# Top-k over 112 candidate sums instead of 256, and V's gate and activation tiles in a pool of their own that opens before U ends

## The chip, the cores and the metric

The kernel runs on 1 core of one Trainium2 chip. The metric is device time in microseconds (us) for one launch, the median of several runs; less is better. Engines are named as in the profile: PE (matrix multiply), PEld (its weight loads), DVE (vector), ACT (scalar), POOL (GpSimd) and SP, which here only issues DMAs. ACTq, SPq and POOLq are the DMA issues in the instruction streams of ACT, SP and POOL.

## What is computed

Two layers of a transformer step on 640 tokens of width 1024, handled as five tiles of 128 tokens (four latent tiles, n = 0 to 3, and one context tile, PT = 4). Each layer has a mixer and then a product-key expert retrieval ("PEER"), which is most of the time and all of the change:

```
q   = (x @ w_q) as 8 heads x 2 halves of 64
sc  = q . sub_keys                       # 128 scores for each token, head and half
sv, si = top_k(sc, 16)                   # 16 best of 128, each half, sorted
cand = sv[half 0][:, None] + sv[half 1][None, :]     # 16 x 16 sums
cv, ci = top_k(cand, 16)                 # 16 best of 256
i1, i2 = si[half 0][ci // 16], si[half 1][ci % 16]
idx  = i1 * 128 + i2                     # one of 16384 experts
gate = softmax(cv)
act  = gelu(u[idx] . x)                  # 8 x 16 = 128 experts for each token
out  = sum over experts of gate * act * v[idx]
```

Both lists of 16 are sorted in falling order. A pair (a, b), with a the rank in half 0 and b in half 1, has at least (a+1)(b+1) pairs (itself among them) with sums no smaller, so a pair can be among the best 16 only where (a+1)(b+1) <= 16. For a < 4 that allows b up to 15, and for a >= 4 it allows b <= 2.

## The kernel before

For the four latent tiles the retrieval is not a gather but dense, in two phases. **U**: for each of 128 chunks of 128 experts, PE multiplies the chunk of u (128x1024) with all 512 latent tokens, three products of hi/lo halves (24 matmuls of 512 columns a chunk), ACT takes the gelu into a tile `ga`, and ACT's queue stores it to DRAM (`gad[c]`). **V**: for each chunk the stored activations are loaded again (tile `gr`), multiplied on DVE with the chunk's gates (tile `gate`, loaded from the DRAM array `Gd`, four chunks a tile), split into hi and lo (tile `whl`, ACT then DVE), and PE multiplies them with the chunk of v (`vh`, `vl`) into eight PSUM banks over all 128 chunks. The weights of either phase come as `raw` and `x` tiles, which live through both phases and are shared, as are their splits `hl`. The context tile uses gathers instead: 128 indirect DMAs by POOL of rows of u (`gather_u`, during U) and of v (`gather_v`, during V), each followed by one pass of DVE.

Where the gates come from: `pick` (line 960) runs once for each of the five tiles. POOL adds the 16 x 16 sums of all 8 heads (line 966), `top16` (lines 953 to 958) makes five DVE passes over each head's sums, small DVE operations split ci into ranks, and for each half DVE compares with a row of 0 to 15 (line 978), POOL multiplies (line 980) and DVE sums (line 981). ACT takes the exponential (line 985). `build_gate` (line 991) turns a tile's result into dense gates: DVE makes one-hot rows E and M (line 1006), PE multiplies them in, ACT copies the product to `stg`, and ACT's queue stores that to `Gd`. The picks of tiles PT and 0 stand ahead of U in the program; the gates of tiles 0 to 3, with the picks of tiles 1 to 3 woven in, are spread over U's chunks 4 to 107 (lines 1201 to 1231).

SBUF is handed out in pools on a stack, by default from the left. Those that matter, in layer l: `q` (through U and V), `a` (`hn`, `ga`, `gth`; U only), `tt` (the picks and gates; until chunk 111 of U, ASPLIT = 112), then `ta` (modulation blocks in four `wm` buffers, in layer 0 alone, two `rowb` rows; the last 16 chunks of U), then after U's last chunk `a` is released and `v` opened, with everything V needs: `gate` 2 buffers of 8 KB a partition, `gr` 6 of 2 KB, `whl` 4 of 4 KB, `gth`, `wm` and `rowb`. The first users of a pool wait until what lay at its place is done.

The order of instructions on each engine and DMA queue is fixed when the program is built: a planner runs through the program with its own costs and, at each point, puts on an engine the earliest instruction in program order that is ready. The chip then runs each engine's list in that order and waits where an operand is late. In V, `issue_after` also ties the multiplication of chunk c to come after the lo split of chunk c - 2 in DVE's list (line 1084).

Of the kernel before, what the change touches and what calls it, by code (L numbers as in the profile page):

```python
# [33 lines left out]
GLD = 4  # L34
# [43 lines left out]
def build(tc, nc, I, O, dbg=None):  # L78
# [39 lines left out]
    def phase(name, wide):  # L118
        if extra[0]:
            extra[0].release()  # L120
        PA[0] = wide
        extra[0] = name and tc.alloc_tile_pool(name=name, bufs=1, space=PSUM, reuse_waits="tile")
# [299 lines left out]
    def mod_steps(P, blocks, bufs):  # L422
        sB = mod_rows(P)
        for l, b in blocks:
            mod_block(P, l, b, sB, bufs)
            yield
# [526 lines left out]
    def top16(s, v, i):  # L953
        V.max(v[:, 0:8], s)  # L954
        V.max_index(i[:, 0:8], v[:, 0:8], s)  # L955
        V.match_replace(s, v[:, 0:8], s, LOWEST)  # L956
        V.max(v[:, 8:16], s)
        V.max_index(i[:, 8:16], v[:, 8:16], s)

    def pick(P, n, sv, si, i1, i2, gt):  # L960
        sif = P.tile([128, 8, 2, 16], F32, name="sif", bufs=1)
        V.tensor_copy(sif, si)
        cv = P.tile([128, 8, 16], F32, name="cv", bufs=1)
        ci = P.tile([128, 8, 16], U32, name="ci", bufs=1)
        cand = P.tile([128, 8, 16, 16], F32, name="cand", bufs=1)
        G.tensor_tensor(cand, sv[:, :, 0, :, None].to_broadcast([128, 8, 16, 16]),
                        sv[:, :, 1, None, :].to_broadcast([128, 8, 16, 16]), OP.add)
        for h in range(8):
            top16(cand[:, h].rearrange("p a b -> p (a b)"), cv[:, h, :], ci[:, h, :])
            yield  # L970
        ab = P.tile([128, 2, 8, 16], U32, name="ab", bufs=1)
        V.tensor_single_scalar(ab[:, 0], ci, 4, OP.logical_shift_right)
        V.tensor_single_scalar(ab[:, 1], ci, 15, OP.bitwise_and)
        abf = P.tile([128, 2, 8, 16], F32, name="abf", bufs=1)
        V.tensor_copy(abf, ab)
        for j, dst in ((0, i1), (1, i2)):
            eq = P.tile([128, 8, 16, 16], F32, name="cand", bufs=1)
            V.tensor_tensor(eq, abf[:, j, :, :, None].to_broadcast([128, 8, 16, 16]),  # L978
                            iota16[:, None, None, :].to_broadcast([128, 8, 16, 16]), OP.is_equal)
            G.tensor_tensor(eq, eq, sif[:, :, j, None, :].to_broadcast([128, 8, 16, 16]), OP.mult)  # L980
            V.tensor_reduce(dst.rearrange("p (h k) -> p h k", h=8), eq, axis=AX.X, op=OP.add)  # L981
            yield
        g3 = gt.rearrange("p (h k) -> p h k", h=8)
        V.tensor_sub(g3, cv, cv[:, :, 0:1].to_broadcast([128, 8, 16]))
        S.activation(gt, gt, AF.Exp)
        z = P.tile([128, 8], F32, name="z", bufs=2)
        V.reduce_sum(z, g3, axis=AX.X)
        V.reciprocal(z, z)
        V.tensor_mul(g3, g3, z[:, :, None].to_broadcast([128, 8, 16]))
# [76 lines left out]
                V.scalar_tensor_tensor(accp, t, dots[:, k:k + 1], accp, op0=OP.mult, op1=OP.add)  # L1066
            yield

    def v_phase(l, P, pv, Gd, gad, steps, mods, finish):
        ws, gt, lows = {}, {}, []  # L1070

        def load_gate(g):
            gt[g] = P.tile([128, 16, GLD, 32], F32, name="gate", bufs=2)
            cc = g * GLD % 64
            load(gt[g], Gd[:, g * GLD // 64, :, cc * 32:(cc + GLD) * 32].rearrange("u p (c t) -> p u c t", c=GLD))

        def prep(c):
            ga = P.tile([128, 512], F32, name="gr", bufs=6)
            load(ga, gad[c])
            if c == 0:  # L1080
                load_gate(0)
            if (c + GAHEAD) % GLD == 0 and c + GAHEAD < NCH:
                load_gate((c + GAHEAD) // GLD)
            with tc.issue_after(lows[-2].ins) if c > 1 else contextlib.nullcontext():
                V.tensor_mul(ga.rearrange("p (u t) -> p u t", t=32), ga.rearrange("p (u t) -> p u t", t=32),  # L1085
                             gt[c // GLD][:, :, c % GLD, :])
            w = P.tile([128, 2, 512], F32R, name="whl", bufs=4)
            lows.append(split(w[:, 0], w[:, 1], ga))
            raw = chunk_tile(c)
            load(raw, I["vC"][l, :, c, :])  # L1090
            vh, vl = hl_tile(), hl_tile()
            split(vh, vl, raw, V)
            ws[c] = (w, vh, vl)
            if True:
                next(steps, None)
                if c % 16 == 15:
                    next(steps, None)
                if c >= MOD0 and (c - MOD0) % 2 == 0:
                    next(mods, None)

        def use(c, n):
            w, vh, vl = ws[c]
            ns = slice(n * 128, (n + 1) * 128)
            p0, q0 = pv[n]
            a, z = c == 0, c == NCH - 1
            h0, h1 = slice(0, 512), slice(512, 1024)
            mm(p0, w[:, 0, ns], vh[:, h0], a, False)
            mm(q0, w[:, 0, ns], vh[:, h1], a, False)
            mm(p0, w[:, 0, ns], vl[:, h0], False, False)
            mm(q0, w[:, 0, ns], vl[:, h1], False, False)  # L1110
            mm(p0, w[:, 1, ns], vh[:, h0], False, z)
            mm(q0, w[:, 1, ns], vh[:, h1], False, z)

        def back(n):
            xs[n] = x_tile(n)
            load(xs[n], xm[l][n])

        for c in range(NCH - TAIL):
            prep(c)
            if c == XLAST:  # L1120
                back(PT)
            for n in range(NL):
                use(c, n)
        for c in range(NCH - TAIL, NCH):
            prep(c)
        for n in range(NL):
            back(n)
        finish(-1)
        E = mybir.EngineType
        with tc.manual_schedule(engines={E.PE, E.DVE, E.Activation, E.Pool}):  # L1130
            for i in range(NL + 2):
                for n in {0: (0,), 1: (1,), 2: (2, 3)}.get(i, ()):
                    for c in range(NCH - TAIL, NCH):
                        use(c, n)
                finish(i)
# [26 lines left out]
    for l in range(DEPTH):  # L1162
# [8 lines left out]
        with tc.tile_pool(name=f"q{l}", bufs=1) as Q:  # L1171
# [9 lines left out]
            with tc.tile_pool(name=f"t{l}", bufs=1) as TP:  # L1181
# [6 lines left out]
                with tc.tile_pool(name=f"tt{l}", bufs=1) as R:  # L1188
# [39 lines left out]
                                next(bg, None)  # L1228
                    for _ in bg:
                        pass  # L1230
            with tc.tile_pool(name=f"ta{l}", bufs=1) as R:
                mods = mod_steps(R, [(0, b) for b in range(40, 48)], 4) if l == 0 else iter(())
                for c in range(ASPLIT, NCH):
                    nc.scalar.dma_start(gad[c], a_chunk(A, l, c))
                    with tc.issue_after(pace[0].ins):
                        next(steps, None)
                    next(mods, None)
                for g in range(2):
                    gate_row(rows[g], l, g, 40, p2())
            A.release()  # L1240
            with tc.tile_pool(name=f"v{l}", bufs=1) as R:
                phase(f"psV{l}", 1)
                wide = [p2(), p2()]
                pv = [(pacc(), pacc()), (p1(), p1())] + [(t[:, :512], t[:, 512:]) for t in wide]
                if dbg and "f" in dbg:
                    load(dbg["f"][l, PT], accp)
                jobs, lgb = {}, []

                def step(n):
                    if n == PT and n not in jobs:  # L1250
                        lgb.extend(bc_row(R.tile([128, D], F32, name="rowb", bufs=2), I[k][l, 1]) for k in ("ln_g", "ln_b"))
                    if n not in jobs:
                        f = (accp,) if n == PT else (pv[n] if n < 2 else (wide[n - 2],))
                        jobs[n] = close_layer(l, R, n, f, rows[grp_of(n)], *lgb)
                    next(jobs[n], None)

                def finish(i):
                    if i < 0:
                        for _ in range(5):
                            step(PT)  # L1260
                        return
                    tile = lambda k: PT if k == -1 else (k if 0 <= k < NL else None)
                    for k in (i - 2, i, i - 1, i, i - 2, i, i - 1, i - 2):
                        if tile(k) is not None and (k >= 0 or i > 0):
                            step(tile(k))

                v_phase(l, R, pv, Gd, gad, gather_v(R, l, idx, gp, dots, accp),
                        mod_steps(R, [(1, b) for b in range(48)], 2) if l == 0 else iter(()), finish)
    phase(None, 0)
    ps_pool.release()  # L1270
    dram.release()
# [99 lines left out]
```

## Time and profile before

| what | value |
|---|---|
| median of 3 runs | 4023.82 us (4019.87 to 4028.7) |
| the profiled execution | 4019.37 us, of which its span is 4017.6 us |
| PE busy | 3791.2 us, 94% of the span |
| DVE busy | 3068.7 us, 76% |
| ACT busy, POOL busy | 1435.9 us (36%), 1218.5 us (30%) |
| mean granted PE clock | 0.969 of full |
| DMA | 934.02 MB, mean 232 GB/s |

Layer 0 has its U from about 517 to 1327.5 us of the span and its V from 1350 to about 2045; layer 1 has them from about 2473 to 3282 and from 3303 on. A busy PE is not PE at its full rate: a matmul counts as busy at either clock.

### The profile page before, as it was taken

What the parts mean: (1) busy time and instruction counts of PE and PEld (TensorE: products, weight loads), DVE (VectorE), ACT (ScalarE), POOL (GpSimd) and SP (SyncE); (2) the same over time, 40 slices, a digit from 0 to 9 for tenths busy, and PEclk for the clock granted to TensorE, in tenths of its full rate; (3) what the DMA queues carried; (4) which work ended last, traced back from release to release, by engine and by line L of the source; (5) the groups of instructions that cost most, each with busy time, mean ns of one, the idle gap of its engine ahead of it and who ended that gap; (6) DMA issues with size and microseconds to landing.
All of it is one profiled execution on the core that took longest, in us unless ns stands there. A gap on an engine that the chain in (4) does not pass through costs nothing. (4 is left out here: it accounts for less than half of the span.)

```text
span 4017.6 us, 52309 instructions
## 1 busy us (share of the span) xinstructions
PE 3791.2 (94%) x18606; PEld 3091.6 (77%) x18606; DVE 3068.7 (76%) x5984; ACT 1435.9 (36%) x2201; POOL 1218.5 (30%) x946
## 2 busy tenths in 40 slices
PE   6799999999999799999999999999999979999998
PEld 5577777777888688888877778777788868888886
DVE  6867799999766588988765659999986537778545
ACT  5443532333333222222344553323343322222222
POOL 5412445442111222322141243553211113343100
PEclk7899999999999899999999999999999989999999
DMA  6223248777888899999831132677788869999763
GB/s 224 79 71 118 84 139 280 251 256 272 292 263 299 298 350 346 342 343 344 261 103 52 58 106 91 237 262 246 243 307 275 263 223 341 348 340 345 251 195 104
DMA packets 405623, 934.02 MB, mean 232 GB/s; under 512 B 32624, under 2 KB 166896, under 8 KB 397168
## 3 DMA queue, kind: packets, MB, share of 16 engines
q1 hardware_dynamic: 280656, 517.34, 39.4%
q0 software_dynamic: 73728, 268.47, 19.0%
q10 hardware_dynamic: 50976, 144.87, 9.7%
q8 instruction: 146, 2.39, 0.2%
q14 instruction: 117, 0.96, 0.1%
HBM read 785.06 MB, written 145.49 MB: 232 GB/s over the span
## 5 line engine op out<-in xcount | busy, mean ns | idle before, releaser
L83 PE MATMUL pa<-Hhi,hl 128*128 128x512 f32 x4096 | 1318.7, 400 | 11.6 <-ACT ga L1044 11.5
L83 PE MATMUL p<-hl,whl 128*128 128x512 f32 x4608 | 1089.3, 390 | 0.0
L83 PEld LDWEIGHTS p<-hl,whl 128*128 128x128 f32 x4608 | 867.5, 188 | 180.3
L83 PEld LDWEIGHTS pa<-Hhi,hl 128*128 128x128 f32 x4096 | 778.9, 191 | 181.5 <-ACT ga L1044 13.9
L83 PE MATMUL pa<-Hlo,hl 128*128 128x512 f32 x2048 | 815.0, 398 | 0.0
L199 ACT ACTIVATE hl<-x 128x1024 fp32r<-128x1024 f32 x284 | 301.3, 1061 | 960.2 <-PE p L83 578.1
L1061 POOL DMA_INDIRECT gth<-v,idx x256 | 361.0, 1410 | 825.2 <-DVE accp L1066 593.6
L199 ACT ACTIVATE hl<-raw 128x1024 fp32r<-128x1024 f32 x292 | 309.0, 1059 | 775.5 <-PE pa L83 373.7
L200 DVE TENSOR_TENSOR hl<-x,hl 128x1024 fp32r<-128x1024 f32 x272 | 345.3, 1270 | 265.6 <-ACT hl L199 260.6
L200 DVE TENSOR_TENSOR hl<-raw,hl 128x1024 fp32r<-128x1024 f32 x246 | 331.2, 1347 | 238.3 <-ACT hl L199 236.2
L83 PEld LDWEIGHTS pa<-Hlo,hl 128*128 128x128 f32 x2048 | 391.3, 191 | 81.5
L83 PE MATMUL pa<-hl,Hhi 128*128 128x512 f32 x1232 | 438.5, 424 | 7.6 <-DVE gtmp L914 2.8
L83 PE MATMUL pa<-hl,whl 128*128 128x512 f32 x1536 | 391.7, 390 | 43.5 <-DMA gr<-gad 22.6
L83 PEld LDWEIGHTS pa<-hl,whl 128*128 128x128 f32 x1536 | 289.2, 188 | 104.2 <-issue 23.0
L1066 DVE SCALAR_TENSOR_TENSOR accp<-gth,dots,accp 128x1024 f32<-128x1024 f32 x254 | 325.3, 1281 | 4.5 <-DMA gth<-v,idx 2.7
L1050 POOL DMA_INDIRECT gth<-u,idx x128 | 165.9, 1296 | 462.9 <-DVE gth L1052 404.9
L1050 POOL DMA_INDIRECT x<-u,idx x128 | 168.9, 1320 | 448.7 <-DVE x L1052 425.6
L83 PEld LDWEIGHTS pa<-hl,Hhi 128*128 128x128 f32 x1232 | 235.4, 196 | 54.9 <-DVE gtmp L914 3.7
L83 PE MATMUL pa<-hl,Hlo 128*128 128x512 f32 x616 | 260.6, 423 | 14.3 <-POOL Hlo L200 10.5
L1006 DVE TENSOR_TENSOR M<-E,g 128x1024 f16<-128x1024 f16 x256 | 189.3, 771 | 58.7 <-PE p L83 57.7
L1024 ACT ACTIVATE stg<-p 128x512 f32<-128x512 f32 x256 | 138.9, 597 | 233.8 <-PE p L83 153.2
L1085 DVE TENSOR_TENSOR gr<-gr,gate 128x512 f32<-128x512 f32 x256 | 175.2, 685 | 24.7 <-DMA gate<-Gd 24.7
(339 smaller groups left out, 4635.6 us busy)
## 6 DMA issues: line engine op xcount, KB each, us to landing
x<-v SPq DMA_DIRECT2D x158, 512.0 KB
raw<-uT SPq DMA_DIRECT2D x130, 512.0 KB
gad<-ga ACTq DMA_DIRECT2D x256, 256.0 KB
Gd<-stg ACTq DMA_DIRECT2D x64, 1024.0 KB
gr<-gad SPq DMA_DIRECT2D x256, 256.0 KB
gate<-Gd SPq DMA_DIRECT2D x64, 1024.0 KB
x<-uT SPq DMA_DIRECT2D x126, 512.0 KB
raw<-v SPq DMA_DIRECT2D x98, 512.0 KB
```

Source lines behind the costliest of these rows:

```text
L83: return T.matmul(out, l, r, start=start, stop=stop, skip_group_check=True)
L199: S.activation(hi, src, AF.Copy)
L200: return (eng or V).tensor_sub(lo, src, hi.bitcast(F32))
L1006: V.tensor_tensor(out, src, col.rearrange("p (q r) -> p q r", r=2)[:, :, None, :].to_broadcast(shape), op)
L1024: S.activation(st[a][:, :, b * 8:(b + 1) * 8], v[:, a], AF.Copy, scale=1.0 / GSCALE)
L1050: G.indirect_dma_start(out=t, out_offset=None, in_=I["u"], in_offset=bass.IndirectOffsetOnAxis(ap=idx[:, k:k + 1], axis=0))
L1061: G.indirect_dma_start(out=t, out_offset=None, in_=I["v"], in_offset=bass.IndirectOffsetOnAxis(ap=idx[:, k:k + 1], axis=0))
L1066: V.scalar_tensor_tensor(accp, t, dots[:, k:k + 1], accp, op0=OP.mult, op1=OP.add)
L1085: V.tensor_mul(ga.rearrange("p (u t) -> p u t", t=32), ga.rearrange("p (u t) -> p u t", t=32), gt[c // GLD][:, :, c % GLD, :])
```

## The change

`pick` adds 4 x 16 sums of the first four ranks (columns 0 to 63 of a head) and 12 x 4 of the other twelve (columns 64 to 111), in two POOL instructions instead of one, and `top16` runs over 112 columns instead of 256. The ranks are then found from the column c: a = max(c >> 4, (c >> 2) - 12), and b = c - min(16 a, 4 a + 48). V's `gate` and `gr` tiles move out of `v` into a pool `H` on the right-hand side, opened after `tt` is released and before `ta`; the other tiles of V stay in `v`. The modulation blocks in `ta` get two buffers instead of four.

```diff
-        cand = P.tile([128, 8, 16, 16], F32, name="cand", bufs=1)
-        G.tensor_tensor(cand, sv[:, :, 0, :, None].to_broadcast([128, 8, 16, 16]),
-                        sv[:, :, 1, None, :].to_broadcast([128, 8, 16, 16]), OP.add)
+        cand = P.tile([128, 8, 256], F32, name="cand", bufs=1)[:, :, :112]
+        for a0, a1, nb in ((0, 4, 16), (4, 16, 4)):
+            shape = [128, 8, a1 - a0, nb]
+            part = cand[:, :, :64] if a0 == 0 else cand[:, :, 64:]
+            G.tensor_tensor(part.rearrange("p h (a b) -> p h a b", b=nb),
+                            sv[:, :, 0, a0:a1, None].to_broadcast(shape),
+                            sv[:, :, 1, None, :nb].to_broadcast(shape), OP.add)
         for h in range(8):
-            top16(cand[:, h].rearrange("p a b -> p (a b)"), cv[:, h, :], ci[:, h, :])
+            top16(cand[:, h], cv[:, h, :], ci[:, h, :])
             yield
...
-        V.tensor_single_scalar(ab[:, 1], ci, 15, OP.bitwise_and)
+        V.tensor_single_scalar(ab[:, 1], ci, 2, OP.logical_shift_right)
         abf = P.tile([128, 2, 8, 16], F32, name="abf", bufs=1)
         V.tensor_copy(abf, ab)
+        cf = P.tile([128, 8, 16], F32, name="cif", bufs=1)
+        V.tensor_copy(cf, ci)
+        V.scalar_tensor_tensor(abf[:, 0], abf[:, 1], -12.0, abf[:, 0], op0=OP.add, op1=OP.max)
+        V.tensor_scalar(abf[:, 1], abf[:, 0], 4.0, 48.0, op0=OP.mult, op1=OP.add)
+        V.scalar_tensor_tensor(abf[:, 1], abf[:, 0], 16.0, abf[:, 1], op0=OP.mult, op1=OP.min)
+        V.tensor_sub(abf[:, 1], cf, abf[:, 1])
...
-            gt[g] = P.tile([128, 16, GLD, 32], F32, name="gate", bufs=2)
+            gt[g] = H.tile([128, 16, GLD, 32], F32, name="gate", bufs=2)
...
-            ga = P.tile([128, 512], F32, name="gr", bufs=6)
+            ga = H.tile([128, 512], F32, name="gr", bufs=6)
...
+            H = tc.alloc_tile_pool(name=f"h{l}", bufs=1, side="right")
             with tc.tile_pool(name=f"ta{l}", bufs=1) as R:
-                mods = mod_steps(R, [(0, b) for b in range(40, 48)], 4) if l == 0 else iter(())
+                mods = mod_steps(R, [(0, b) for b in range(40, 48)], 2) if l == 0 else iter(())
...
+            H.release()
```

## Rows read from the trace of the kernel before

**Rows 1.** Stretches: us; busy (count) of PE, PEld, DVE, ACT, POOL; PEclk, DMA, GB/s.

```profile
640.00:905.00 265.00, 243.68 (x1214) 194.79 (x1213) 262.60 (x458) 87.15 (x121) 126.06 (x62) 0.96 0.74 254
905.00:1327.50 422.50, 415.52 (x2360) 338.75 (x2358) 298.57 (x428) 156.79 (x234) 75.82 (x62) 1.00 0.80 275
1327.50:1350.10 22.60, 0.01 (x1) 0.01 (x1) 2.72 (x4) 4.41 (x6) 4.68 (x5) 0.59 0.90 291
1400.00:1950.00 550.00, 550.00 (x2428) 455.56 (x2427) 482.45 (x652) 159.65 (x202) 156.17 (x109) 1.00 0.98 342
2595.00:2880.00 285.00, 259.28 (x1290) 207.31 (x1289) 284.94 (x471) 92.43 (x129) 132.37 (x65) 0.95 0.73 246
```

**Rows 2.** Waits of PE, whole run: us in total, times, longest.

```profile
PE p L83 <- DVE M L1006: 40.1, 18, 3.9
PE pa L83 <- ACT ga L1044: 11.5, 4, 5.4
```

**Rows 3.** Timeline at layer 0's change from U to V: start, us, engine, instruction [idle].

```profile
1328.89 0.33 ACTq L1234 DMA_DIRECT2D gad<-ga  x1
...
1331.24 0.33 SPq L1079 DMA_DIRECT2D gr<-gad  x1
...
1349.39 0.63 ACT L199 ACTIVATE whl<-gr 128x512 fp32r<-128x512 f32 x1 [10.81 <-DVE gr L1085]
...
1350.12 2.04 PE L83 MATMUL pa<-hl,whl 128*128 128x512 f32 x4 [22.61 <-DMA gr<-gad]
```

**Rows 4.** The same of layer 1.

```profile
3285.59 0.33 SPq L1079 DMA_DIRECT2D gr<-gad  x1
...
3302.30 0.63 ACT L199 ACTIVATE whl<-gr 128x512 fp32r<-128x512 f32 x1 [18.86 <-DVE gr L1085]
...
3302.98 2.08 PE L83 MATMUL pa<-hl,whl 128*128 128x512 f32 x4 [20.90 <-ACT whl L199]
```

**Rows 5.** Timeline of SP's queue in layer 0: the first load for V.

```profile
1274.07 0.33 SPq L1090 DMA_DIRECT2D raw<-v  x1
```

**Rows 6.** Timeline of layer 0's U: last modulation block, first gate row.

```profile
1275.11 0.16 DVE L429 TENSOR_TENSOR modT<-modT,bmod 128x2 f32<-128x2 f32 x1
...
1284.31 1.02 ACT L439 ACTIVATE g2row<-p 128x1024 f32<-128x1024 f32 x1
```

**Rows 7.** Waits of ACT in V of layer 0, 1400 to 1950 us.

```profile
ACT hl L199 <- PE p L83: 389.8, 101, 3.9
```

**Rows 8.** Instructions on tile cand: duration ns min/median/max, first and last start us, forms.

```profile
L954 DVE MAX8 cv<-cand x80: 401/406/425, 550.7 to 2812.0; 128x8 f32<-128x256 f32 x80
...
L955 DVE FIND_INDEX8 ci<-cv,cand x80: 408/420/439, 553.4 to 2818.1; 128x8 uint32<-128x256 f32 x80
...
L980 POOL TENSOR_TENSOR cand<-cand,sif x20: 4567/4964/6827, 571.1 to 2871.4; 128x2048 f32<-128x2048 f32 x20
...
L966 POOL TENSOR_TENSOR cand<-sv x10: 3670/3694/3797, 547.0 to 2801.5; 128x2048 f32<-128x2048 f32 x10
```

**Rows 9.** The same for tile sc, whose passes run over 128 columns.

```profile
L954 DVE MAX8 sv<-sc x160: 274/331/584, 453.4 to 2497.6; 128x8 f32<-128x128 f32 x160
...
L955 DVE FIND_INDEX8 si<-sv,sc x160: 290/350/598, 454.6 to 2499.9; 128x8 uint32<-128x128 f32 x160
```

**Rows 10.** Groups of DVE, 480 to 1010 us: busy us, mean ns | idle.

```profile
L975 DVE CAST abf<-ab 128x256 f32<-128x256 uint32 x5 | 1.5, 303 | 0.0
```

**Rows 11.** Timeline at the start of tile 2's pick, layer 0.

```profile
762.51 3.69 POOL L966 TENSOR_TENSOR cand<-sv 128x2048 f32<-128x2048 f32 x1 [1.42 <-DVE i L981]
762.55 4.80 DVE L1006 TENSOR_TENSOR M<-E,g 128x1024 f16<-128x1024 f16 x2
...
766.81 0.23 PE L83 MATMUL p<-M,E 128*128 128x128 f16 x1 [1.38 <-DVE M L1006]
```

**Rows 12.** Timeline of ACT at the context tile's pick, layer 0 and layer 1.

```profile
568.00 0.31 ACT L985 ACTIVATE gp<-gp 128x128 f32<-128x128 f32 x1 [8.70 <-DVE gp L984]
...
2523.89 0.31 ACT L985 ACTIVATE gp<-gp 128x128 f32<-128x128 f32 x1 [10.13 <-DVE gp L984]
```

More of the change, by code (lines that the diff above doesn't have):

```diff
@@ L1067, in gather_v, with v_phase @@
             yield
-    def v_phase(l, P, pv, Gd, gad, steps, mods, finish):
+    def v_phase(l, P, H, pv, Gd, gad, steps, mods, finish):
         ws, gt, lows = {}, {}, []
         def load_gate(g):
-            gt[g] = P.tile([128, 16, GLD, 32], F32, name="gate", bufs=2)
+            gt[g] = H.tile([128, 16, GLD, 32], F32, name="gate", bufs=2)
             cc = g * GLD % 64
@@ L1265, in finish @@
                             step(tile(k))
-                v_phase(l, R, pv, Gd, gad, gather_v(R, l, idx, gp, dots, accp),
+                v_phase(l, R, H, pv, Gd, gad, gather_v(R, l, idx, gp, dots, accp),
                         mod_steps(R, [(1, b) for b in range(48)], 2) if l == 0 else iter(()), finish)
+            H.release()
     phase(None, 0)
```

## The prediction

> **What bounds the kernel now.** I read the page's busy times first, then the stretches, then who PE waits for, then the timelines where it waits. PE is the engine to watch: in V it is busy without a gap for 550 of 550 us at full clock [rows 1]. It loses time in two kinds of place in each layer. At the change from U to V it stands still for 22.6 us in layer 0 and 20.9 us in layer 1 [rows 3, 4]. And in the stretch of U where the picks and gates are made it is busy for 243.7 of 265 us in layer 0 and 259.3 of 285 us in layer 1, while DVE is busy for 262.6 and 284.9 us of these: DVE sets the pace there, and PE loses 21.3 and 25.7 us [rows 1], mostly to the one-hot rows M (40.1 us in 18 waits over the run, [rows 2]). The two parts of the change fall on these two places.
>
> **The change of phase.** The last chunk's store is issued at 1328.89, and the first load of `gr` goes out 2.35 us later, at 1331.24 [rows 3]: that is when the pool `v` opens. All that follows is a chain of load, multiplication and split, which ends in ACT's hi split at 1349.39 and PE's start at 1350.12. With `gate` and `gr` in `H`, the loads and the first two multiplications can run during U's last chunks, and the chain from the opening is only the split, since `whl` still lies in `v`: 1350.12 - 1349.39 = 0.73 us. So PE starts at about 1331.24 + 0.73 = 1331.97 instead of 1350.12 and saves 18.1 us. In layer 1 it starts at 3285.59 + (3302.98 - 3302.30) = 3286.27 instead of 3302.98 and saves 16.7 us [rows 4]. Sum: 34.8 us, with bounds 0 (the planner leaves the loads where they are) and 34.8. I take the upper end, because the planner already issues loads of V when a place is free: the first of v's chunks goes out at 1274.07, 53 us before U's end [rows 5]. I leave 2 us off for V's first chunks, where DVE must now also take in the first gathered rows of v while PE is already running. The clock I leave alone: it is at a mean of 0.59 over the idle stretch [rows 1], and a remaining gap of 4 us may still bring it to its lower level.
>
> What is moved costs this. SP gets eight loads ahead of U's last ones, six of 256 KB and two of 1 MB, 3.5 MB or 10.2 us at the 342 GB/s of V [rows 1]. In U's last 422 us the DMA engines are busy to 0.80 [rows 1], so some 84 us are free, and these loads hide there; a u chunk that comes later by 10 us is covered by the chunks already split (ten `hl` tiles, two a chunk). DVE gets two multiplications more before U's end, where it is busy for 298.6 of 422.5 us [rows 1], so they cost nothing. With two `wm` buffers instead of four the eight modulation blocks may take longer; they end at 1275.11, and the first row made of them is copied at 1284.31 [rows 6], which gives 9.2 us of cover. Bounds 0 and some 5 us; I take 0.
>
> **The picks.** MAX8 takes at least 401 ns over 256 columns and 274 over 128, FIND_INDEX8 408 and 290 [rows 8, 9]: 122 ns for 128 columns, so 138 ns for the 144 that go. There are 5 passes (the other three taken alike) x 8 heads = 40 a tile: 5.5 us. The five added operations have half the width of the cast at line 975, which takes 303 ns [rows 10]: between 0.5 and 1.5 us, of which I take the upper end. Net 4.0 us of DVE time a tile. The sums on POOL go from 2048 elements in 3.69 us [rows 8] to 896 in two instructions: 1.6 us by their number, 3.7 if a short inner row of 4 costs what it saves; I take 1.7, nearest to the row by its time an element. That matters to DVE, since it stands while POOL adds: at 762.55 two M operations are begun and end 1.15 us after POOL's 3.69 us are over, and PE, which needs an M, waits 1.38 us [rows 11]. So another 2.0 us a tile (bounds 0 and 2.1). Together 6.0 us a tile, 30 us a layer, 60 us in all, of DVE time. POOL's two products at line 980 (4.96 us each, [rows 8]), which halt DVE as well, stay.
>
> [...]
>
> How much reaches PE? Tiles 1 to 3 lie in the stretch where DVE sets the pace: 18 us a layer. If DVE's list were the only limit, PE's loss of 21.3 and 25.7 us would fall by 18 each. If the waits came from the halts by line 980 alone, they would stay. I take 11 a layer, a little over half, since DVE has no idle time there to absorb a halt: 22 us. Tiles PT and 0 lie ahead of it, where PE waits only at the context tile's exponential. ACT waits for it for 8.70 and 10.13 us with everything behind it in its list, the gelu among it [rows 12], and PE for up to 5.4 us of that (11.5 us in four waits, [rows 2]), so 10.13 - 5.4 = 4.7 us are covered. DVE's chain ahead of it gets 5.5 + 2.0 = 7.5 us shorter, but the planner, which sees a shorter chain too, may put the exponential earlier. Between 0 and 11.5 us; I take 5.
>
> **Sum.** 34.8 - 2 + 22 + 5 = 60 us. The profiled execution took 4019.4 us, 4.4 less than the median of the three runs; from it 3959.4 comes out, from the median 3963.8. I say 3961.
>
> **Rivals.**
> - The picks' relief doesn't reach PE, because the halts by line 980 set its waits: the change of phase alone, 33 us, 3987 us. For it: the waits are short (40.1 us in 18) and each can follow a halt. Against it: DVE has no idle time in between. 0.14.
> - All of it does: 34.8 - 2 + 36 + 11.5 = 80 us, 3940 us. For it: DVE busy for 284.9 of 285 us. 0.13.
> - V of layer 0 is bound by the DMA engines (busy to 0.98 there), so an earlier start ends it earlier only by the 3.5 MB already loaded, 10.2 us instead of 18.1: 3969 us. Against it: ACT's splits wait 389.8 us for PE to free tiles, in 101 waits, and for no DMA [rows 7]. 0.07. [...]
> - The change doesn't do what it says: the loads stay behind U's end, for want of a place or by the planner's order. With the picks' 27 us 3994 us (0.04); with little of these either about 4020 us (0.03).
> - Slower: the exponential moves ahead on ACT. Its place in ACT's list comes from the planner's costs, and there are five a layer, of which one now makes PE wait. If each of the ten waited W us, PE would lose 10 x (W - 4.7), against some 10 now. It decides from W = 4.7 + (34.8 - 2 + 22 + 10)/10 = 11.2 us; at W = 13 PE would lose 83 us and the kernel would take about 4039 us. For it: both such waits of today are near it (8.7 and 10.1). Against it: the chain on DVE gets shorter, and the later tiles' exponentials cause no wait today. 0.05.
>
> **How the numbers follow.** My forecast has 0.54, with a range of its own of 3945 to 3978. The rivals' 3940, 3969, 3987 and 3994 are all faster by more than 0.2% (8 us, about what a measurement of this kernel can tell from no change): 0.54 + 0.14 + 0.13 + 0.07 + 0.04 = 0.92; within 0.2% 0.03; slower 0.05. The range for 8 in 10 reaches from 3931, where the clock also gives something back, to 3994.
>
> **What would show it.** Right: loads of `gr` and `gate` on SP's queue some 50 us or more before U's end, PE idle for 4 to 6 us at both changes of phase, MAX8 over 112 columns at about 0.26 us, the sums on POOL at 1.6 to 2.0 us in two parts, and fewer waits of PE for M. Wrong: `gr` loads that start with `v`; PE idle again a few chunks into V, on `whl` or a load; new waits of ACT at line 985; a DVE stretch as long as before. If U's waits are unchanged, the second part of the sum fails; if V waits for DMAs, the first.

## The result, and the profile after

The changed kernel took 3981.72 us (median; 3979.86 to 3985.91), the kernel before beside it 4021.85 us. The ratio is 0.9899, with a 95% interval of 0.9882 to 0.9916: 40 us, or 1.0%, less. 3961 was predicted, so the gain is two thirds of the 60 us forecast. The profiled execution took 3980.8 us, 38.6 less than that of before; its span is 3979.0 us.

I give the stretches between the starts of the first and last matmul of each phase, and PE's idle time between the phases, read from the two traces, since the page shows only sums over the run:

| stretch | before | after | difference |
|---|---|---|---|
| U, layer 0 | 826.3 | 830.0 | +3.7 |
| PE's wait from U to V, layer 0 | 22.6 | 4.4 | -18.2 |
| V, layer 0 | 699.5 | 699.7 | +0.2 |
| U, layer 1 | 824.9 | 817.6 | -7.3 |
| PE's wait from U to V, layer 1 | 20.9 | 4.2 | -16.7 |
| V, layer 1 | 698.5 | 698.5 | 0 |

The stretches of the changed kernel that answer to [rows 1], and one more, 1216 to 1250 us, columns as there:

```profile
640.00:905.00 265.00, 245.86 (x1370) 197.19 (x1369) 263.82 (x508) 95.72 (x139) 100.02 (x61) 0.98 0.75 259
905.00:1330.00 425.00, 414.81 (x2231) 338.55 (x2231) 267.04 (x390) 149.54 (x218) 69.65 (x61) 0.99 0.81 276
...
1216.00:1250.00 34.00, 25.66 (x107) 20.44 (x105) 15.41 (x24) 11.31 (x12) 5.76 (x5) 0.90 1.05 367
1400.00:1950.00 550.00, 550.00 (x2428) 455.44 (x2427) 485.76 (x647) 159.59 (x202) 163.97 (x113) 1.00 0.98 345
2595.00:2880.00 285.00, 267.19 (x1557) 215.22 (x1556) 283.68 (x541) 109.60 (x163) 95.42 (x59) 0.98 0.77 265
```

V is what it was: 2428 matmuls in 550 us before and after. In the stretch of the picks DVE is as full as before (263.8 of 265 us). New are 34 us, 80 us before the end of layer 0's U, in which PE is busy for only 25.7, at a clock of 0.90.

PE's waits over the whole run, to be set beside [rows 2]:

```profile
PE p L83 <- DVE M L1016: 33.4, 20, 3.9
PE pa L83 <- ACT ga L1054: 22.0, 8, 8.1
...
PE pa L83 <- ACT whl L199: 8.6, 2, 4.4
```

The waits for M fell by 6.7 us only. Those for the gelu's tile `ga` doubled, and one of them is 8.1 us long.

The change from U to V in the timeline, layer 0 and then layer 1, beside [rows 3, 4]:

```profile
1218.73 0.43 SPq L1089 DMA_DIRECT2D gr<-gad  x1
...
1332.16 0.33 ACTq L1245 DMA_DIRECT2D gad<-ga  x1
...
1334.45 0.63 ACT L199 ACTIVATE whl<-gr 128x512 fp32r<-128x512 f32 x1 [2.32 <-DMA gad<-ga]
...
1335.18 1.19 PE L83 MATMUL pa<-hl,whl 128*128 128x512 f32 x2 [4.40 <-ACT whl L199]
...
3263.68 1.15 ACT L199 ACTIVATE whl<-gr 128x512 fp32r<-128x512 f32 x2 [2.17 <-DMA gad<-ga]
...
3264.36 2.07 PE L83 MATMUL pa<-hl,whl 128*128 128x512 f32 x4 [4.20 <-ACT whl L199]
```

`gr` is loaded from 1218.73 on, 112 us before U ends (1330.78). What is left of the chain is what the prediction left: `v` opens when the last store has freed its place, 2.3 us after that was issued, and PE starts 0.73 us after ACT's split (1335.18 - 1334.45).

The timeline of the new stall, on SP, ACT and PE:

```profile
1216.83 1.86 SPq L308 DMA_DIRECT2D wm<-wmodT  x2
1218.73 0.43 SPq L1089 DMA_DIRECT2D gr<-gad  x1
1220.10 0.38 SPq L1085 DMA_DIRECT2D gate<-Gd  x1
1221.05 9.54 SPq L1089 DMA_DIRECT2D gr<-gad  x1
...
1223.80 0.58 ACT L1054 ACTIVATE ga<-pa 128x512 f32<-128x512 f32 x1
1235.51 0.33 ACTq L1233 DMA_DIRECT2D gad<-ga  x1
1235.87 1.28 ACT L302 ACT_TABLE_LOAD   x1 [11.49 <-DMA gate<-Gd]
...
1242.08 0.79 PE L83 MATMUL pa<-Hhi,hl 128*128 128x512 f32 x1 [8.05 <-ACT ga L1054]
```

The gelu of a chunk ends at 1224.4, but its store goes out at 1235.51, and what ended ACT's 11.49 us of idle time is the landing of the first `gate` load, issued at 1220.10 on SP. The store has no data in common with that load. In the trace the DMAs of SP and ACT take their completion semaphores (the counters that tell that a transfer has landed) from one set of eight in turn (numbers 100 to 104, 106, 109 and 110 in the issues from 1216.78 us on), and the store's is the one that the `gate` load holds, number 109: ACT's wait for it ends at 1235.45. But for its own gelu the store waits for nothing else. The load is 1 MB and lands only after 15.4 us (1220.10 to 1235.51), at a time when `wm`, `rowb`, `gate` and `gr` loads are under way together (DMA share 1.05 in the stretch). ACT waits in its issue of the store. Behind it in ACT's list stand a split, the work on the `rowb` rows and two table loads (1.28 us each), so the next gelu comes only at 1241.42, and PE with it.

In layer 1 the store of the same chunk waits in the same way, but its semaphore, number 102, is held by a `gr` load of 256 KB issued at 3159.53. ACT's wait is 6.21 us, and no work on `rowb` follows:

```profile
3172.72 1.06 ACT L199 ACTIVATE hl<-raw 128x1024 fp32r<-128x1024 f32 x1 [6.21 <-DMA gr<-gad]
```

There PE has no wait from 3140 to 3200 us.

The exponentials: tile 0's in ACT's timeline of the kernel before, to be set beside [rows 12],

```profile
625.61 0.31 ACT L985 ACTIVATE gt<-gt 128x128 f32<-128x128 f32 x1 [4.45 <-DVE gt L984]
```

and ACT's timeline and then PE's of the changed kernel:

```profile
557.50 0.31 ACT L995 ACTIVATE gp<-gp 128x128 f32<-128x128 f32 x1 [4.51 <-DVE gp L994]
...
600.98 0.31 ACT L995 ACTIVATE gt<-gt 128x128 f32<-128x128 f32 x1 [9.21 <-DVE gt L994]
...
604.20 0.79 PE L83 MATMUL pa<-Hhi,hl 128*128 128x512 f32 x1 [4.46 <-ACT ga L1054]
...
2546.01 0.80 PE L83 MATMUL pa<-Hhi,hl 128*128 128x512 f32 x1 [4.53 <-ACT ga L1054]
```

ACT's wait at the context tile (`gp`) fell from 8.70 to 4.51 us and is covered now. At tile 0 (`gt`) it rose from 4.45 to 9.21 us, as the exponential there starts 24.6 us earlier in layer 0, and PE waits 4.5 us behind it in either layer.

The instructions on tile `cand`, beside [rows 8] (L969 is the old line 966, L990 the old 980):

```profile
L954 DVE MAX8 cv<-cand x80: 252/256/279, 548.5 to 2748.7; 128x8 f32<-128x112 f32 x80
...
L955 DVE FIND_INDEX8 ci<-cv,cand x80: 256/266/276, 549.5 to 2754.7; 128x8 uint32<-128x112 f32 x80
...
L969 POOL TENSOR_TENSOR cand<-sv x20: 885/1179/1973, 546.5 to 2742.2; 128x512 f32<-128x512 f32 x10, 128x384 f32<-128x384 f32 x10
...
L990 POOL TENSOR_TENSOR cand<-cand,sif x20: 4529/5429/6628, 562.0 to 2802.5; 128x2048 f32<-128x2048 f32 x20
```

Each of the 400 passes is about 0.15 us shorter, as forecast. The sums are not: by the trace their two instructions take 2.7 us a tile in the mean (from 885 to 1973 ns each) instead of 3.7, where 1.7 was taken. One halt by POOL's product, in layer 0 of the changed kernel:

```profile
696.08 5.41 POOL L990 TENSOR_TENSOR cand<-cand,sif 128x2048 f32<-128x2048 f32 x1 [1.67 <-DVE cand L988]
696.99 5.65 DVE L1016 TENSOR_TENSOR M<-E,g 128x1024 f16<-128x1024 f16 x2
702.09 0.23 PE L83 MATMUL p<-M,E 128*128 128x128 f16 x1 [3.00 <-DVE M L1016]
```

Two M operations, 0.69 us each elsewhere, take 5.65 us beside a POOL product of 5.41 us that began first, and PE stands for 3.00 us. DVE counts as busy all the while. That made "DVE is full" a bad measure: part of that time it was standing.

How much can be added up from the traces, as the time by which DVE operations that overlap a POOL operation of the picks outlast the median of their own kind (line and shape; only where that is over 0.3 us; no view shows this sum). Beside the product it is 80.1 us in 19 operations before and 79.7 us in 18 after, so 19 and then 18 of the 20 products hold DVE up; beside the sums it is 27.7 us before and 10.8 after. In the stretch 620 to 880 us the two make 37.4 us before and 35.7 after, and the same in 2560 to 2820 us. The longest and the median of M in the kernel before:

```profile
L1006 DVE TENSOR_TENSOR M<-E,g x256: 654/687/5479, 702.0 to 3152.8; 128x1024 f16<-128x1024 f16 x128
```

### The profile page after: what moved, and what is told of

Its sections match the earlier page's. It is cut to its first block, busy times and chain, and to the rows that moved or that the text cites. A ratio compares the mean times of both kernels' runs of the same rounds, so it can differ in the third digit from the quotient of the medians.

```text
span 3979.0 us, 52325 instructions
## 1 busy us (share of the span) xinstructions
PE 3775.0 (95%) x18606; PEld 3079.3 (77%) x18606; DVE 3000.7 (75%) x6034; ACT 1434.6 (36%) x2201; POOL 1182.6 (30%) x956
## 4 chain that ended last, share of the span: by engine, by line
PE 69%; DVE 18%; issue 3%; ACT 2%; DMA 2%; POOL 1%; ACTq 0%; POOLq 0%; SPq 0%; DVEq 0%
PE pa L83 37%; PE p L83 30%; DVE hl L200 2%; DVE M L1016 2%; DVE gth L1062 2%; PE sx L83 2%; DVE x L1062 2%; DVE E L1016 1%; DVE si L955 1%; DVE sc L956 1%; DMA gad<-ga 1%; DVE si L958 1%; DVE cand L988 1%; DVE sv L954 1%; DVE sv L957 0%
## 5 line engine op out<-in xcount | busy, mean ns | idle before, releaser
L200 DVE TENSOR_TENSOR hl<-raw,hl 128x1024 fp32r<-128x1024 f32 x246 | 306.5, 1247 | 219.3 <-ACT hl L199 217.6
L1060 POOL DMA_INDIRECT gth<-u,idx x128 | 148.3, 1158 | 475.0 <-DVE gth L1062 407.8
L1060 POOL DMA_INDIRECT x<-u,idx x128 | 148.8, 1162 | 467.8 <-DVE x L1062 418.0
L1016 DVE TENSOR_TENSOR M<-E,g 128x1024 f16<-128x1024 f16 x256 | 199.0, 802 | 104.1 <-PE p L83 103.1
L200 DVE TENSOR_TENSOR whl<-gr,whl 128x512 fp32r<-128x512 f32 x256 | 177.0, 691 | 12.1 <-ACT whl L199 12.1
```

The lines of the kernel that those rows point to most:

```text
L200: return (eng or V).tensor_sub(lo, src, hi.bitcast(F32))
L1016: V.tensor_tensor(out, src, col.rearrange("p (q r) -> p q r", r=2)[:, :, None, :].to_broadcast(shape), op)
L1060: G.indirect_dma_start(out=t, out_offset=None, in_=I["u"], in_offset=bass.IndirectOffsetOnAxis(ap=idx[:, k:k + 1], axis=0))
```

## Experiments

Diffs are against the changed kernel unless said. Ratios are to the kernel before, timed on the same chip; it took 4019 to 4020 us there.

### The change in its two parts, and the stall

**Only the pool** (the change without its edit of `pick`):

> The pool H alone, with the picks as before (256 sums). The changed kernel's profile: both changes of phase save together 34.9 us, and a stall of PE of 8.2 us near 1242 us (layer 0, 16 chunks before U's end) with a stretch at the lower clock gives some 11 us back. If that stall belongs to H's early loads, this kernel shows it too and gains 23 to 25 us on the kernel before (about 3995 us on the profiled run's 4019). If the stall comes from the picks' new order, this kernel has no such stall and gains 33 to 35 us.

Measured 3994.14 us, ratio 0.9936 (0.9923 to 0.995): 26 us. PE's waits from U to V are 4.4 and 4.2 us, and the same stall of PE on `ga` is there (8.0 us, at 1254.86). It belongs to the pool, not to the picks.

**Only the picks** (the kernel before, with the new `pick`; V as it was):

> The picks alone (112 sums), pools and modulation buffers as before. If the two parts of the change add up, this gains what is left of the changed kernel's 39 us after the pool's 23 to 26: 13 to 17 us, about 4005. If the picks only pay together with the earlier start of V, it gains below 8 us; if the prediction's 27 us for the picks held and the pool's part hid some of it, 24 to 30 us.

Measured 4008.62 us, ratio 0.9967 (0.9955 to 0.998): 10 us by the medians, 13 by the ratio. U is 8.8 and 7.2 us shorter. With the 26 of the pool that makes 36 to 39 us: the parts add up, and neither hides the other.

**V's first loads later on SP**, behind U's last load:

```diff
-        load(raw, I["uT"][l, c])
+        last_u[0] = load(raw, I["uT"][l, c])
...
-            load(gt[g], Gd[...])
+            with tc.issue_after(last_u[0].ins) if g < 2 else contextlib.nullcontext():
+                load(gt[g], Gd[...])
...
-            load(ga, gad[c])
+            with tc.issue_after(last_u[0].ins) if c < 6 else contextlib.nullcontext():
+                load(ga, gad[c])
```

> The changed kernel, but the first two gate loads and the first six gr loads are put behind the load of the last u chunk on SP's list (some 50 us later). Theory S: near 1235 us a store of ga on ACT's queue waits for the semaphore that the first gate load holds, which takes 15 us to land because eight loads (3.5 MB) go out at once beside the modulation blocks; ACT and then PE stand behind it. Then the stall of 8.2 us goes, the gaps at the changes of phase stay at 4 to 5 us, and it gains 8 to 12 us on the changed kernel's 3981: about 3971. Rival: ACT waits for the two rowb loads anyway (they wait for the release of the pool of the gates), as before at 1235 us: then the stall stays at over 4 us and the gain is below 4 us.

Measured 3972.4 us, ratio 0.9886 (0.9871 to 0.9901). That is 9 us less than the change by the medians and 5 by the ratios, whose intervals overlap, so the gain does not stand on the times alone; the stretch shows it. The same 34 us in this kernel:

```profile
1216.00:1250.00 34.00, 34.00 (x151) 27.82 (x150) 23.46 (x36) 14.07 (x16) 7.60 (x7) 1.00 0.98 366
```

The DMA engines move as much (366 GB/s beside 367), PE waits for nothing, and 151 matmuls are done instead of 107. At 34/151 = 0.225 us each the 44 are worth 9.9 us; U of layer 0 took 820.6 us, 9.4 less. So it was not the amount of DMA traffic. The wait of ACT's stores for the `gate` loads is still there, later and shorter:

```profile
1271.44 1.06 ACT L200 ACTIVATE hl<-x 128x1024 fp32r<-128x1024 f32 x1 [7.53 <-DMA gate<-Gd]
```

Another, of 5.67 us, comes behind it, but PE waits for `ga` for only 1.1 us from 1180 to 1320. It takes a long wait, or one with more of ACT's work behind it, to reach PE; which of the two matters more was not tried.

### What the picks' relief ran into

Three explanations stood against each other: the waits come from halts by POOL's product (H); they come from DVE's time, of which too little was saved (T); or they come from POOL being busy at all.

**POOL's product to DVE:**

```diff
-            G.tensor_tensor(eq, eq, sif[:, :, j, None, :].to_broadcast([128, 8, 16, 16]), OP.mult)
+            V.tensor_tensor(eq, eq, sif[:, :, j, None, :].to_broadcast([128, 8, 16, 16]), OP.mult)
```

> The changed kernel with the product eq * sif (two per tile, 4.5 to 6.6 us on POOL) on DVE (2.3 us each). Theory H (halts): PE's waits in U come from the moments in which DVE stands because POOL runs that product, for which the order of the lists has no room; 20 of 20 gone, the waits for M fall from 33.4 us to below 15 and the two waits of 4.6 us behind the exponential go: 20 to 35 us faster than 3981, 3946 to 3961. Theory T (DVE time): PE's waits follow DVE's total time in the stretch; DVE wins about 2.7 us x 10 a layer, and as the picks' 30 us a layer gave PE 7.5, this gives 7 a layer: 14 us, about 3967.

Measured 3914.61 us, ratio 0.9748 (0.9727 to 0.9768): 67 us less than the change by the medians and 61 by the ratios, about twice what was expected of H, although DVE was given 20 products of 2.28 us more (46 us, for 80 us of halts). U took 798.1 and 784.0 us. PE's waits for M, 33.4 us in the change, are now

```profile
PE p L83 <- DVE M L1016: 1.1, 1, 1.1
```

The waits behind the exponentials, which H had expected to go as well, stayed: PE's waits for `ga` are 21.1 us in all, with the stall of the change among them.

**The same, with DVE's comparison ahead of it done twice** (that much useless work on DVE):

```diff
-            V.tensor_tensor(eq, abf[:, j, ...], iota16[...], OP.is_equal)
+            for _ in range(2):
+                V.tensor_tensor(eq, abf[:, j, ...], iota16[...], OP.is_equal)
```

> As the product on DVE, and the comparison before it is done twice (2.3 us more on DVE for each of the 20, same result), so that DVE's time is again about that of the changed kernel, but planned work instead of halts. Theory H: within 8 us of the kernel with the product on DVE, so 3950 to 3969. Theory T: back at about 3981.

Measured 3919.46 us, ratio 0.9749 (0.9735 to 0.9763): no difference that can be told.

**The product on DVE, with the old 256 sums** (the edit of `pick` taken back):

> The pool H and the product on DVE, with the picks over 256 sums: DVE gets back the 30 us a layer that the shorter picks saved, in planned work (but also POOL's longer sums, 3.7 us a tile, which halt DVE). Theory H (only the halts count): 0 to 10 us slower than the product on DVE with 112 sums (3914.6), so 3915 to 3925. Theory T (DVE time counts): the 15 us that the picks gave before, or up to 60: 3930 to 3975.

Measured 3919.46 us, ratio 0.9758 (0.9745 to 0.9772). Without the product on POOL, the shorter picks are worth some 4 us by the ratios, within the intervals.

**POOL kept busy with memsets**, which write and don't read (60 in all), with the product on DVE:

```diff
             eq = P.tile([128, 8, 16, 16], F32, name="cand", bufs=1)
+            for _ in range(MS):      # MS = 3
+                G.memset(eq, 0.0)
```

> The product on DVE, and POOL fills the tile eq with zeros three times (some 1.8 us each by the 0.31 us of 256 elements) ahead of each comparison: POOL is as busy as with the product, but reads nothing from SBUF. Result unchanged, since the comparison overwrites the tile. Theory H, with halts from POOL's reads alone: within 8 us of 3914.6. Rival G: PE's waits came from POOL being taken up (gathers and sums behind the product), or DVE stands whatever POOL does: 3955 to 3981.

Measured 3922.2 us, ratio 0.9763 (0.975 to 0.9777): 6 to 8 us more than without the memsets, with overlapping intervals.

The stretch 2560 to 2820 us, columns as in [rows 1], of the change:

```profile
2560.00:2820.00 260.00, 236.17 (x1224) 188.51 (x1223) 260.00 (x487) 87.33 (x124) 113.49 (x65) 0.97 0.74 251
```

with the product on DVE:

```profile
2560.00:2820.00 260.00, 260.00 (x1439) 209.79 (x1438) 254.95 (x520) 101.50 (x145) 75.31 (x55) 1.00 0.82 281
```

with the comparison done twice as well:

```profile
2560.00:2820.00 260.00, 260.00 (x1389) 209.00 (x1388) 260.00 (x512) 98.31 (x139) 83.44 (x58) 1.00 0.82 280
```

and with the memsets, here and in layer 0:

```profile
620.00:880.00 260.00, 254.37 (x1362) 203.75 (x1361) 257.19 (x517) 95.39 (x135) 121.01 (x84) 1.00 0.83 287
2560.00:2820.00 260.00, 257.81 (x1406) 206.44 (x1405) 256.83 (x517) 98.51 (x141) 103.75 (x75) 0.99 0.81 281
```

In the third fence DVE is busy for 260.00 of 260 us and PE too: a DVE without a gap costs PE nothing, so T falls. With the memsets POOL is busy for 121 us of layer 0's stretch (the change: 110.7) and PE for 254.4 (the change: 237.0), so a busy POOL alone is not it. Nor is it that the product's chain became shorter on DVE: comparison and product took 2.28 + 5.43 = 7.7 us with the product on POOL and 3 x 2.28 = 6.8 us where the comparison is done twice, and that second comparison cost nothing that can be told. What PE feels is the single operation that stands. The operations M in the change (duration ns min/median/max):

```profile
L1016 DVE TENSOR_TENSOR M<-E,g x256: 630/685/5403, 668.8 to 3131.1; 128x1024 f16<-128x1024 f16 x128
```

and with the product on DVE:

```profile
L1016 DVE TENSOR_TENSOR M<-E,g x256: 633/685/694, 675.1 to 3073.7; 128x1024 f16<-128x1024 f16 x128
```

The median stays; only the longest falls, from 5403 to 694 ns. The timeline of the kernel with the memsets has two M beside POOL in the same way as at 696.08 above:

```profile
715.19 5.54 POOL L990 MEMSET cand<- 128x2048 f32 x3 [1.05 <-DVE i L994]
715.65 1.27 DVE L1019 TENSOR_TENSOR M<-E,g 128x1024 f16<-128x1024 f16 x2
```

POOL is busy for 5.54 us, and the two M that begin half a microsecond later take 1.27 us together, where they took 5.65 beside the product. (M's longest in that kernel is 1.54 us; POOL still has its sums there, which read.) The memsets are not without effect on DVE: a cast with one input, 0.28 us long by its median, began 0.39 us after one of them, at 557.17, and took 1.98 us.

So two M took 5.65 us beside POOL's product, which reads two tiles, and 1.27 beside its memsets, which read none. That the reads make the difference is my inference from these two figures: the product and the memsets are also different operations, and no run parts that. In 16 of the 18 halts of the change the product had begun first; in the other two M's record begins 0.31 us ahead of the product's (788.45 and 2730.33) and M stood all the same, for 5.40 us, so which record begins first does not tell which of the two stands.

That the gain was 61 to 67 us and not the 33.4 us of waits for M has two sources in the rows. PE's idle time in the stretch went from 260 - 236.17 = 23.8 us to none in layer 1, and from 23.0 to 1.1 us in layer 0: waits for other things behind a halted DVE were in it too. And the clock went from 0.97 to 1.00, by which 260 us are worth some 8 us a layer, if PE's rate goes with its clock: behind layer 0's change of phase in the changed kernel PE did 6 matmuls in 2 us at 0.50 (1336 to 1340) and 10 or 11 at 1.00 (1342 to 1352). Together that is an estimate of some 61 us.

### Towards the best version

**Late loads, product and sums on DVE:** the diffs of the late loads and the product, and

```diff
-            G.tensor_tensor(part.rearrange("p h (a b) -> p h a b", b=nb),
+            V.tensor_tensor(part.rearrange("p h (a b) -> p h a b", b=nb),
```

> The changed kernel with H's first loads behind the last u load, the product on DVE and the candidate sums on DVE too (no two-input work of POOL left in the picks). The late loads gave 9 us on the changed kernel, the product 67; if they add up 3905, and the sums' halts (1.1 and 0.9 us, ten times) are worth another 0 to 6: 3899 to 3906. If the product's gain already held the late loads', 3912.

Measured 3909.1 us, ratio 0.9732 (0.9719 to 0.9746), slower than the 3899 to 3906 expected. The longest of PE's waits for `ga` are now behind the two exponentials of the context tile, 5.9 us each, at 562 and 2461 us: they had moved back there.

**The same with the sums left on POOL:**

> H's first loads behind the last u load and the product on DVE, sums on POOL. If late loads and product add up: 3905. Beside the kernel with the sums on DVE as well (3909) it tells what the sums' place is worth: with halts of 1.1 and 0.9 us, 0 to 6 us slower than that one if even short halts count; the same or faster if they don't.

Measured 3907.4 us, ratio 0.9715 (0.9698 to 0.9733): the place of the sums is worth nothing, with halts of about 1 us.

**The context tile's exponential behind the gelu of chunk 20**, added to the version with the sums on DVE. Its gates aren't needed before V:

```diff
+        if n == PT:
+            return
+        soften(P, gt)
+
+    def soften(P, gt):
+        g3 = gt.rearrange("p (h k) -> p h k", h=8)
         S.activation(gt, gt, AF.Exp)
...
-        S.activation(ga, ps, AF.Gelu_apprx_tanh)
+        last_g[0] = S.activation(ga, ps, AF.Gelu_apprx_tanh)
...
                         nc.scalar.dma_start(gad[c], a_chunk(A, l, c))
+                        if c == 20:
+                            with tc.issue_after(last_g[0].ins):
+                                soften(R, gp)
```

> The kernel with late loads, product and sums on DVE (3909.1), where PE still waits for 6.0 us in each layer behind the context tile's exponential; here that exponential (with its sum and division) is put behind the gelu of chunk 20 on ACT's list. Theory E (ACT's list, in which the exponential stands too early): both waits go, 12 us and up to 6 us from the clock: 3891 to 3898. Rival: another tile's exponential or the gelu itself stalls ACT then, as in the changed kernel, where the wait moved from the context tile to tile 0: above 3903.

Measured 3903.56 us, ratio 0.9707 (0.9688 to 0.9726): 116 us (2.9%) below the kernel before, the lowest median of all. PE's waits for `ga` in the kernel without this step:

```profile
PE pa L83 <- ACT ga L1055: 15.7, 4, 5.9
```

and with it:

```profile
PE pa L83 <- ACT ga L1062: 5.7, 6, 1.6
```

10 us of waits went, and U is 5.6 and 5.3 us shorter in the profiled runs. The times show 4 to 5.5 us against the two kernels above, with overlapping intervals, and 11 to 18 were expected: the trace carries this step, the times alone don't. ACT still waits at tile 0's exponential, for 6.02 and 5.32 us.

### A miss: `whl` in the right-hand pool too

The 4.4 us that are left at the change of phase are the wait of `whl` for its place, so `whl` went into `H` in the version with late loads and sums on DVE:

```diff
-            w = P.tile([128, 2, 512], F32R, name="whl", bufs=4)
+            w = H.tile([128, 2, 512], F32R, name="whl", bufs=4)
```

> As the kernel with late loads, product and sums on DVE (3909.1), with V's whl tiles in H as well. The prediction had the remaining gap at the change of phase (4.4 us in each layer) down to whl lying in v, which opens when the last store has landed. If so the gap falls to 1 to 2 us (the last gelu must still free a PSUM bank), and the lower clock after it goes: 6 to 12 us, 3897 to 3903. Rival: PE waits for the PSUM banks or the phase's release as long: gap above 3.5 us, 3907 to 3911.

Measured 3951.04 us, ratio 0.9825 (0.9808 to 0.9843): 37 us more by the ratios. The gap did go; V's first matmuls now stand among U's last ones. But V's own matmuls became slower. V in this kernel, columns as in [rows 1]:

```profile
1600.00:1700.00 100.00, 100.00 (x430) 80.60 (x429) 87.06 (x120) 27.65 (x37) 28.00 (x20) 1.00 0.97 341
...
3500.00:3600.00 100.00, 100.00 (x430) 80.55 (x430) 77.19 (x82) 28.22 (x36) 41.11 (x28) 1.00 0.97 339
```

and with `whl` in `v`:

```profile
1600.00:1700.00 100.00, 100.00 (x443) 82.82 (x442) 90.96 (x130) 28.50 (x37) 28.22 (x19) 1.00 0.98 345
...
3500.00:3600.00 100.00, 100.00 (x443) 82.82 (x442) 78.64 (x83) 29.09 (x38) 39.09 (x29) 1.00 0.97 344
```

PE is full and its clock 1.00 in both, but 430 matmuls are done in 100 us instead of 443: 0.2326 us each instead of 0.2257, in both layers. Over 128 chunks of 24 matmuls that is 21 us a layer, 42 in all, more than the gaps of the change of phase had left to give. In the trace successive matmuls start 231 and 235 or 236 ns apart in turn, where with `whl` in `v` they start 226 or 227 ns apart. Why is open: the instructions are the same, the places of `whl` (which holds the weights of these matmuls), `gr` and `gate` in SBUF are others, and so is the order in which V begins. Nothing was run that parts these.

**Both, the late exponential and `whl` in `H`:**

> Both of the two before it, the late exponential and the whl tiles in H. If they add up, which they should as they lie 700 us apart in each layer: 3880 to 3892; if one of them fails, its own rival's price above that.

Measured 3943.61 us, ratio 0.981 (0.9791 to 0.9828), far above the 3880 to 3892 that the two together were to give. The late exponential is worth 6 to 7 us here too, and V's slower matmuls stay.

## Why the prediction was right in direction and a third too large

**The change of phase (34.8 us): right.** 18.2 + 16.7 = 34.9 us of PE's wait went. PE starts 0.73 and 0.68 us after the split that stands at the opening of `v`; 0.73 and 0.68 were taken.

**V's first chunks (-2 us): not seen.** V's lengths agree to 0.2 us.

**The moved loads, taken at nothing: this step failed in layer 0.** The prediction looked for what could be late on SP's own queue (a u chunk, the modulation blocks) and found cover for each; the cover held, as PE waits for nothing but `ga` from 1180 to 1320 us. (The eight loads are 3.67 MB, 10.7 us at 342 GB/s, not 3.5 MB and 10.2 us; nothing hangs on it.) It did not look at which other engine waits for a completion of these loads. ACT's store did, for 11.1 us, and that cost 9.4 us of the 18.2 won there (830.0 - 820.6, U of layer 0 with and without it). In layer 1, where the store meets a `gr` load instead and no `wm` and `rowb` loads go out beside it, ACT waits for 6.21 us and PE doesn't. Which load a store meets was luck: the program's turn through the semaphores decides it. The prediction asked what waits behind these loads, not what waits for their completion. The run with the late loads showed it by taking the stall away.

**The picks (22 us): the mechanism was the first rival's, and the size came out between.** DVE's passes became shorter as forecast. The sums on POOL, taken at 2.0 us less a tile, became 1.0 us shorter, and what DVE lost in the sums' halts fell (27.7 to 10.8 us), but the product's halts, the larger part, stayed (80.1 and 79.7). I let a little over half of that reach PE because DVE had no idle time. But DVE's time was not the limit: the busy DVE of [rows 1] contained the halts, and a DVE with still more work cost PE nothing once the product was gone from POOL. What the shorter picks did give, some 13 us over both layers (7.3 in layer 1; 826.3 - 820.6 = 5.7 in layer 0 with the stall taken away), comes with 6.7 us less of waits for M and with a clock of 0.98 instead of 0.96 and 0.95 in the stretch; how much each of them gives was not taken apart. The rival's 0.14 for "set by the halts" was too low: the row that told it, M of 4.80 us beside POOL's 3.69 us [rows 11], had been read as a price of the sums, and the product, longer and twice a tile, was left standing as something that doesn't change.

**The exponential (5 us): failed; nothing was won.** PE's waits for `ga` outside the stall are 22.0 - 10.2 = 11.8 us, against 11.5 before. The wait moved from the context tile to tile 0. That is the mechanism of the rival on the slow side, in small: the order, planned with other costs, puts another exponential too early, and PE's long wait went only where a tie (the late exponential) put one later.

So: 34.9 + 13.0 - 9.4 = 38.5 us, against 38.6 between the two profiled runs. This restates the table of stretches and is no second proof of it; that the two parts are worth 26 and 10 to 13 us is shown by the runs that have one of them alone.

## What to carry to other kernels

Before an engine is taken for the limit because it is full, look at the longest of its operations beside their median: a few that are eight times too long may be halts. Here they were, and it paid to remove what halted them rather than to shorten the rest. When loads are moved to an earlier place, ask not only what they push back on their queue but which engines wait for a completion that they hold. Where a planner fixes the order of engines, a shorter chain moves its waits elsewhere, so tie what must not come early.

## What the runs showed of the hardware that was not expected

- Two DVE operations of 0.69 us on two SBUF tiles each took 5.65 us beside a POOL product of 5.41 us, which reads SBUF; the first of them ended 0.55 us after it. Beside three memsets of 5.54 us together the same two took 1.27. In the changed kernel 18 of the 20 products held up such an operation, one of 128 x 128 (line 985, 0.28 us by its median) for 4.61 us.
- A DVE cast with one input, of 0.28 us, took 1.98 us beside POOL's memsets.
- The DVE product takes 2.28 us where POOL takes 5.43 us (median), so moving it to the "full" engine shortened its chain as well.
- A store of 256 KB on ACT's queue stood until a load of 1 MB on SP's queue had landed, and ACT was idle for 11.49 us; no data tied them.
- The same V matmuls run at 0.2257 or 0.2326 us each at full clock with PE never idle, by the version of the kernel. The cause is open.
